# A decoder layer on one core: half 0's output products begin in rooms that half 0 of x leaves, and projections in another order

## The chip, the cores and the metric

The kernel runs on one core of one Trainium2 chip. The metric is the time of one execution on the device, in microseconds (us), as the median of several runs. A core has five engines that work side by side: TensorE (PE) for matrix products, with its own step for loading the stationary operand (PEld in the profile), VectorE (DVE), ScalarE (ACT), GpSimd (POOL), and SyncE (SP), which here only issues transfers (DMAs). Each engine works through its own queue in order and waits on semaphores for the others. SBUF is the memory on the chip, PSUM holds the results of PE in eight banks of 128 x 512 values.

## The reference

One layer for a sequence of 1024 positions and a width of 1024, in float32. What counts for this kernel:

```python
h = rms_norm(x, ln_pre_mix[l])
proj = h @ w_in[l]                      # pool input (256) | q | k | v (12 heads of 64 each)
q, k = rope(q, pos), rope(k, pos)
pool_out = multi_scale_pool(u_pool, w_pool[l], pool_scale[l])
attn_out = dilated_attention(q, k, v)   # windows (128,1), (512,4), (2048,16), merged by softmax denominators
mix = concatenate([pool_out, attn_out]) @ w_out[l]
x = x + rms_norm(mix, ln_post_mix[l])
h = rms_norm(x, ln_pre_ffn[l])
f = (silu(h @ w_gate[l]) * (h @ w_up[l])) @ w_down[l]
x = x + rms_norm(f, ln_post_ffn[l])
```

## The kernel before

**Split numbers.** Every large product is computed three times over split operands: a float32 value is kept as a high part, which PE takes as it is (type fp32r), and the low rest, and high x high, high x low and low x high are added up in PSUM (`PASSES`, three matmuls per step). So each weight tile has to be split before it is used: `wtile` (line 441) loads it, ACT copies the high part and POOL or DVE subtracts (`split`, line 432). The table `we` says for each projection whether DVE or POOL subtracts.

**Halves, pairs and units.** The sequence is cut into two halves of 512 positions (h = 0, 1), the twelve heads into six pairs (p = 0 to 5). One pair and one half is a *unit*: units 0 to 7 are pairs 0 to 3 with both halves in turn, 8 and 9 are pairs 4 and 5 of half 0, and 10 and 11 are pairs 4 and 5 of half 1. Within a unit: `scores` (line 883; eight steps of several products `ps_s<-k,qh` and `ps_s<-k,ql`, half of the steps with every fourth query as stationary operand, "side 1"), `merge` (the weights of the branches), `weigh` (line 973; sixteen scalings of the exponents by DVE, ACT or POOL, by the table `wu`), `turn` (line 1022; transposes through PE, `ps_t<-idt,pp` and `ps_t<-pmt,pp`) and `product` (line 1039; `ps_o<-ptr,v`). The turns may be preceded by transposes of the identity that nobody reads (`ps_t<-idt`); the table `dm` has their number for a unit and a turn.

**Projections as filler.** x, normalised by rows and split, lies in eight tiles `xk[0..7]` of 128 x 2 x 1024 (high and low, all positions). While the units run, the query, key and value projections of the later pairs are the filler of PE: `Fill` (line 717) is a list of steps, and `pull` takes the next step from the list that is current. `await_` (line 694) pulls steps in front of a product whose operands are planned to be late, and the table `x` adds some at single places. A step of a query or key projection (`proj_half`, line 740) is one matmul of 512 columns; a step of a value projection (`v_rows`, line 776) is two matmuls of 256 columns. Split weights lie in tiles `whl`, of which there are two; a value projection needs both, a query or key projection one.

**The order.** A plan in fractions of units is written out by hand: `put(steps, from, to)` spreads steps between two times, such as 10.45 (45 hundredths into unit 10), and `emit` (line 1133) sorts all of them into one program order. PE keeps that order. The other engines' queues are ordered by the framework's planner on the basis of its own estimates. All loads here go through the queue of SP.

**Output products.** The mixed heads of a pair and a half go to memory (`mixd`). `mixed(h)` (line 1242) loads them back as operands k = 0 to 7 (0 and 1 are the pooling part, 2 to 7 the pairs), and `out_proj` (line 1260) multiplies them with the eight output blocks d = 0 to 7. For half 0 they are filler as well, from 10.4487 on: blocks 0 to 2 with operands 2, 3, 4, 5, 0, 1 and 6 up to 11.1989, then operand 7 and the blocks after. Their operands get new tiles in the places of `xk[2]`, `xk[3]`, `xk[6]` and `xk[7]` (`room`, line 1253).

**After the units.** The output products of half 1 and the two norms follow (`chain`, line 1384), then the SwiGLU part, whose matrices are multiplied by blocks with seven products in place of eight (`seven`, line 1567; P1 to P7), and the down projection in the same manner (`down`, line 1834). The last norm needs the mean of the squares of each column: `End` (line 1761) adds squares on DVE into `sq`, keeps the last one apart in `jk`, and `finish` (line 1787) sums both over the partitions by one-column products with `ones` on PE.

Of the kernel before, what the change touches and what calls it, by code (L numbers as in the profile page):

```python
# [35 lines left out]
 'we': (1, 1, 1, 1, 0, 0, 0, 0, 0, 1, 0, 1),  # L36
 'nt0': 0.4937,
 'nt1': 0.5402,
# [3 lines left out]
 'lt': 2.594,  # L42
 'ls': 2.229,
 'lm': 2.364,
 'lw': (3.3, 0.494),
 'nm': 0.0429,
 'n2': -0.0544,
 'n0': 0.2179,
 'n1': 0.3788,
# [24 lines left out]
 'own': {0: {'s0': 0.559,  # L74
             's1': 0.6524,
             'm': 0.8373,
             'w0': 0.8763,
             'w1': 1.2254,
             't0': 1.0833,
             'v0': 1.254,  # L80
# [3 lines left out]
              't1': 1.7207,  # L84
              'v1': 1.9549,
              's1': 0.5395,
              'w0': 0.9014,
              's0': -0.0018,
              'm': 0.6753,
              't0': 0.9791,  # L90
              'v0': 1.0941},
         4: {'m': 0.7142,
             'w0': 0.7313,
             'w1': 0.9854,
             't1': 1.7615,
             'v0': 1.3193,
             'v1': 2.0088,
             's1': 0.4336,
             's0': -0.0464,
             't0': 0.8576},  # L100
         8: {'t1': 1.7086,
             'w1': 0.8589,
             'v0': 1.1186,
             's1': 0.5245,
             'w0': 0.6843,
             'v1': 1.7349,
             'm': 0.612,
             's0': -0.0747,
             't0': 0.7884},
         9: {'s0': -0.0903,  # L110
             't1': 1.7717,
             'v1': 2.0108,
             'w1': 0.9638,
             'w0': 0.6643,
             'v0': 1.1804,
             's1': 0.4339,
             't0': 0.8982,
             'm': 0.543},
         3: {'s0': -0.23,
             't1': 1.7219,  # L120
             'w0': 0.6301,
             'v0': 1.0706,
             's1': 0.6,
             'w1': 1.5566,
             'm': 0.5165,
             'v1': 2.0672},
         1: {'t0': 0.9112,
             'w0': 0.7177,
             'v0': 1.0955,
             'w1': 1.2073,  # L130
             't1': 1.8557,
             'm': 0.5413,
             's0': -0.0064,
             's1': 0.5555,
             'v1': 1.9757},
         10: {'t1': 1.5392,
              't0': 0.9708,
              'v1': 1.9193,
              's1': 0.5967,
              'w1': 1.1507,  # L140
              'v0': 1.1197,
              'w0': 0.6922,
              's0': 0.0404,
              'm': 0.6285},
         6: {'s1': 0.337,
             't1': 1.9316,
             'v0': 1.2209,
             'v1': 2.0292,
             'w1': 1.1291,
             'm': 0.5238,  # L150
             's0': 0.0204,
             'w0': 0.66,
             't0': 0.812},
         7: {'w0': 0.6456,
             't1': 1.8658,
             'm': 0.6436,
             't0': 0.8534,
             's1': 0.4768,
             'v1': 2.0764,
             'v0': 1.1321,  # L160
             'w1': 1.534,
             's0': -0.0044},
         5: {'s1': 0.6462,
             'v1': 2.0851,
             'w1': 1.1017,
             'w0': 0.6388,
             'v0': 1.1233,
             'm': 0.6104,
             't1': 1.8076,
             's0': -0.0052,  # L170
             't0': 1.0214},
         2: {'t1': 1.8214,
             'm': 0.553,
             'w0': 0.7076,
             's0': 0.0298,
             'v1': 2.0119,
             'w1': 1.0298,
             'v0': 1.3523,
             't0': 0.8098}},
 'vt': ((1.029, 1.2775), (2.6607, 3.2018), (4.97, 5.5237), (6.9389, 7.4289), (8.9599, 10.3692), (9.9449, 10.0423)),  # L180
 'pw': 0.2539,
 'pm': (0.8885, (0.8136, 0, 0), (0.8661, 1, 0), (1.035, 0, 1), (1.06, 1, 1)),
# [7 lines left out]
 'lr': (9.8402, 9.7125, 10.0044, 10.2503),  # L190
 'lw0': (9.8553, 10.4888),
 'lc': (12.2353, 12.0824, 11.9907, 12.2417),
 'o0': 10.4487,
 'o1': 11.1989,
 'o2': 12.6671,
 'np': 11.8844,
 'z0': 12.5886,
 'z1': 14.1924,
 'c0': (0.0502, 0.087, 0.2602, 0.595, 0.2709, 0.6193, -0.3497, 0.4162, 0.0467, 0.0316),
 'cut': 5,  # L200
 'ew': (0.1691, 0.4576),
 'c1': (0.115, 0.228, 0.4967, 0.7534, 0.4979, 0.8562, 1.4605, 1.6658, 1.0598, 1.0489),
 'c2': ((1.1162, 1.3893), (1.2471, 1.9662)),
 'e0': ((0.26, 0), (0.42, 0), (0.47, 0.9)),
 'ea': (0, 2, 4),
 'e1': (1.12, 1.25, 1.8, 1.2, 1.5),
 'wu': {(8, 7): 1,
        (6, 10): 1,
# [3 lines left out]
        (6, 7): 0,  # L212
        (0, 0): 0,
        (8, 8): 0,
        (10, 3): 0,
        (0, 1): 0,
        (0, 13): 0,
        (8, 2): 2,
# [8 lines left out]
        (4, 3): 2,  # L227
        (9, 1): 2,
        (10, 11): 2,
        (10, 12): 1,  # L230
        (7, 7): 2,
        (7, 11): 1,
        (10, 6): 1,
        (10, 4): 2,
        (5, 10): 2,
        (10, 15): 2,
        (1, 9): 0,
        (9, 6): 2,
        (2, 13): 2,
        (2, 3): 2,  # L240
        (4, 11): 0,
        (2, 4): 1,
        (2, 9): 2,
        (2, 10): 2,
        (2, 2): 0,
        (8, 6): 2,
        (10, 8): 2,
# [3 lines left out]
        (8, 11): 0,  # L251
# [4 lines left out]
        (8, 5): 0,  # L256
        (8, 10): 2,
        (8, 13): 2,
        (0, 10): 2,
        (6, 14): 2,  # L260
        (0, 5): 2,
        (1, 10): 2,
        (10, 9): 0,
        (4, 14): 2,
        (11, 10): 0,
        (11, 2): 2,
# [6 lines left out]
        (11, 6): 2,  # L273
# [5 lines left out]
        (11, 5): 0,  # L279
# [3 lines left out]
        (6, 6): 2,  # L283
        (10, 13): 2,
        (10, 0): 2,
        (3, 5): 2,
        (3, 9): 2,
        (2, 15): 1,
        (10, 2): 2,
        (1, 5): 0,  # L290
        (10, 7): 2,
        (11, 4): 2,
        (9, 2): 0,
        (9, 14): 0,
        (9, 13): 0,
        (10, 10): 1,
        (2, 8): 2,
        (2, 5): 2,
        (0, 6): 2,
        (0, 15): 1,  # L300
        (0, 8): 0,
        (0, 14): 2,
        (0, 3): 1,
# [73 lines left out]
def hybrid_block(ctx: ExitStack, tc: tile.TileContext, xT, w_in, w_v, w_pv, w_pool, w_out, w_gate, w_up, w_down,  # L377
# [875 lines left out]
    def room(h, n):  # L1253
        if h:
            return fw([P, 2, 2, 512], F32R)
# [763 lines left out]
```

## Time and profile before

| | us |
|---|---|
| median of three runs | 1132.08 |
| the three runs | 1132.82, 1132.08, 1131.9 |
| profiled execution: its own time | 1132.82 |
| its span, first to last instruction | 1131.0 |
| PE busy | 1121.3 |
| DVE, POOL, ACT busy | 779.7, 578.8, 568.0 |

The granted clock of PE was 1.00 throughout. The stages in the profile's time: first projections up to about 85 us, the units from there to about 430 us, norms and the first SwiGLU blocks to about 560 us, then products without a gap up to about 1100 us, and the end.

In the timeline a row has the start and the length in us, the engine, the line, the operation, the tile written and the tiles read, the shape and the number of merged instructions; in brackets stands idle time before it and what ended it. Lengths of matmuls overlap, since they are pipelined, so what one costs is read from start to start. A row of a group has count, busy time, mean ns of one, and idle time of the engine before them. A row of a window has, after its length, busy us and instructions of PE, PEld, DVE, ACT and POOL, the clock, the share of the DMA engines and GB/s. A row of DMA issues has count, KB each and the median us from issue to landing; GB/s there stands in 40 slices of the stretch.

### The profile page before, as it was taken

How to read it: one execution, taken by the hardware profiler on the slowest of the kernel's cores; microseconds unless marked ns; L12 is line 12 of the kernel's file. 1: busy time of each engine (PE TensorE's matmuls, PEld its weight loads, DVE VectorE, ACT ScalarE, POOL GpSimd, SP SyncE). 2: the span in 40 equal slices, each digit the busy share in tenths (PEclk: the TensorE clock that was granted, in tenths of full speed). 3: DMA queues.
4: the chain of work that ended last, by engine and by line, in shares of the span. 5: the costliest groups of instructions: out<-in, count | busy, mean ns of one | idle time of the engine just before them, and what ended most of it. 6: DMA issues, size and time to landing. Idle time of an engine off the chain costs nothing.

```text
span 1131.0 us, 16700 instructions
## 1 busy us (share of the span) xinstructions
PE 1121.3 (99%) x5881; PEld 966.6 (85%) x5881; DVE 779.7 (69%) x1461; ACT 568.0 (50%) x1102; POOL 578.8 (51%) x484
## 2 busy tenths in 40 slices
PE   9999999999999999999999999999999999999997
PEld 7889999999999888878888888888888888888897
DVE  7877878687888666979566755675557365454594
ACT  7457777776787775855323223232232436343430
POOL 0302535363665023232678655976576977655531
PEclk9999999999999999999999999999999999999999
DMA  7324151515137358320345334544454769766642
GB/s 277 127 93 155 57 168 57 167 57 180 48 129 299 130 206 300 131 107 29 141 166 204 139 141 158 218 161 176 162 195 165 273 216 364 248 200 192 204 168 75
DMA packets 85364, 189.01 MB, mean 167 GB/s; under 512 B 8736, under 2 KB 23584, under 8 KB 83872
## 3 DMA queue, kind: packets, MB, share of 16 engines
q1 hardware_dynamic: 84992, 187.68, 47.2%
q8 instruction: 46, 0.75, 0.3%
q14 instruction: 38, 0.31, 0.1%
q10 hardware_dynamic: 288, 0.27, 0.1%
HBM read 134.96 MB, written 52.95 MB: 166 GB/s over the span
## 4 chain that ended last, share of the span: by engine, by line
PE 92%; DVE 2%; POOL 2%; issue 1%; ACT 1%; DMA 1%; DVEq 0%; POOLq 0%; SPq 0%; ACTq 0%
PE ps_pj L382 33%; PE ps_o L382 23%; PE ps_s L382 23%; PE ps_t L382 8%; PE ps_t L385 3%; POOL whl L1610 1%; POOL fw L1610 1%; DVE sq L1365 1%; DVE z L1397 0%; DMA wraw<-in_w_up_dram 0%; DVE z L1398 0%; DMA rw<-in_w_up_dram 0%; POOL whl L437 0%; POOL y L1811 0%; ACT z L1416 0%
## 5 line engine op out<-in xcount | busy, mean ns | idle before, releaser
L382 PE MATMUL ps_pj<-x,whl 128*128 128x512 f32 x480 | 140.0, 406 | 0.0
L1610 POOL TENSOR_TENSOR fw<-rw,fw 128x512 fp32r<-128x512 f32 x74 | 101.2, 1392 | 61.9 <-ACT fw L1608 61.9
L382 PE MATMUL ps_o<-tT,fw 128*128 128x512 f32 x504 | 117.8, 389 | 0.4 <-DVE p L1645 0.4
L382 PEld LDWEIGHTS ps_o<-tT,fw 128*128 128x128 f32 x504 | 94.5, 188 | 20.4 <-DVE p L1645 0.9
L437 POOL TENSOR_TENSOR whl<-wraw,whl 128x512 fp32r<-128x512 f32 x50 | 67.6, 1371 | 83.1 <-ACT whl L433 55.7
L988 POOL TENSOR_SCALAR pp<-pp,wv 128x256 f32<-128x256 f32 (+1 forms) x98 | 47.0, 498 | 116.5 <-DVE wv L966 69.2
L930 ACT ACTIVATE pp<-pp,sx 128x128 f32<-128x128 f32 (+1 forms) x192 | 89.4, 467 | 32.1 <-DVE sx L927 31.4
L1610 POOL TENSOR_TENSOR whl<-rw,whl 128x512 fp32r<-128x512 f32 x42 | 62.1, 1504 | 61.5 <-ACT whl L1608 61.5
L382 PEld LDWEIGHTS ps_pj<-x,whl 128*128 128x128 f32 x480 | 85.0, 189 | 9.8
L1608 ACT ACTIVATE fw<-rw 128x1024 fp32r<-128x1024 f32 x37 | 38.5, 1056 | 92.9 <-DVE rw L1576 32.5
L1757 POOL TENSOR_TENSOR op<-rw,op 128x512 fp32r<-128x512 f32 x38 | 60.3, 1586 | 36.4 <-ACT op L1756 35.0
L1756 ACT ACTIVATE op<-rw 128x1024 fp32r<-128x1024 f32 x38 | 40.2, 1060 | 66.5 <-DMA rw<-bd 29.0
L382 PE MATMUL ps_pj<-whl,x 128*128 128x256 f32 (+1 forms) x432 | 73.0, 303 | 0.0
L1036 DVE TENSOR_TENSOR ptr<-ps_t,ptr 128x512 fp32r<-128x512 f32 (+1 forms) x84 | 55.9, 666 | 17.6 <-ACT ptr L1035 17.1
L382 PE MATMUL ps_pj<-b,fw 128*128 128x512 f32 x264 | 61.6, 389 | 0.0
L382 PEld LDWEIGHTS ps_pj<-whl,x 128*128 128x128 f32 x432 | 59.9, 191 | 1.8
L1035 ACT ACTIVATE ptr<-ps_t 128x512 fp32r<-128x512 f32 (+1 forms) x84 | 48.3, 575 | 23.6 <-PE ps_t L385 20.7
L656 POOL TENSOR_TENSOR rsw<-rsw,sinr 128x512 f32<-128x512 f32 x19 | 24.9, 1312 | 65.6 <-DVE rsw L654 58.7
L382 PEld LDWEIGHTS ps_pj<-b,fw 128*128 128x128 f32 x264 | 49.6, 188 | 10.3
L382 PE MATMUL ps_o<-ptr,v 128*128 128x128 f32 (+1 forms) x472 | 56.2, 254 | 0.0
L382 PEld LDWEIGHTS ps_o<-ptr,v 128*128 128x128 f32 x472 | 52.1, 163 | 3.1 <-DVE ptr L1036 0.3
L382 PE MATMUL ps_s<-k,qh 128*128 128x128 f32 (+1 forms) x192 | 53.4, 290 | 0.0
(342 smaller groups left out, 2926.0 us busy)
## 6 DMA issues: line engine op xcount, KB each, us to landing
rw<-bd SPq DMA_DIRECT2D x77, 256.0 KB, 4.7
v<-vd SPq DMA_DIRECT2D x22, 512.0 KB, 4.7
rw<-wsd SPq DMA_DIRECT2D x44, 256.0 KB, 4.1
rw<-in_w_gate_dram SPq DMA_DIRECT2D x20, 512.0 KB, 3.6
rw<-in_w_up_dram SPq DMA_DIRECT2D x20, 512.0 KB, 4.6
bd<-p SPq DMA_DIRECT2D x33, 256.0 KB, 3.2
rw<-in_w_down_dram SPq DMA_DIRECT2D x33, 256.0 KB, 4.8
fw<-in_w_down_dram SPq DMA_DIRECT2D x16, 512.0 KB, 4.1
```

What stands on the lines that cost most here:

```text
L382: return tc.keep_in_program_order(nc.tensor.matmul(*a, **k))
L385: return tc.keep_in_program_order(nc.tensor.transpose(dst, src, by))
L437: parts.append(eng.tensor_tensor(dst[:, 1, at:at + w], src[:, at:at + w], dst[:, 0, at:at + w].bitcast(F32), ALU.subtract))
L656: pin(eng[0].tensor_tensor(s, s, sinr[:, sl], ALU.mult))
L930: nc.scalar.activation(pt[:, j, lo:], pt[:, j, lo:], AF.Exp, bias=sx[:, 0, side, j, hd, 0:1], scale=-1.0, accum_out=sx[:, 0, side, j, hd, ...
L988: nc.gpsimd.tensor_scalar(pv, pv, un.wv[:, side, j, hd:hd + 1], 1.0, op0=ALU.mult, op1=ALU.mult)
L1035: nc.scalar.activation(ptr[:, 0, :w], t[:, :w], AF.Copy)
L1036: nc.vector.tensor_tensor(ptr[:, 1, :w], t[:, :w], ptr[:, 0, :w].bitcast(F32), ALU.subtract)
L1608: nc.scalar.activation(w[n][:, :, 0], raw[n], AF.Copy)
L1610: low[0] = nc.gpsimd.tensor_tensor(w[n][:, i, 1], raw[n][:, i], w[n][:, i, 0].bitcast(F32), ALU.subtract)
L1756: nc.scalar.activation(w[:, :, 0], raw, AF.Copy)
L1757: nc.gpsimd.tensor_tensor(w[:, 0, 1], raw[:, 0], w[:, 0, 0].bitcast(F32), ALU.subtract)
```

## The change

- **Rooms.** The operands of half 0's output products no longer get new tiles in the places of whole x tiles. They are loaded into halves of them: operands 2 to 5 into the columns of half 0 of `xk[2]`, `xk[3]`, `xk[6]`, `xk[7]`, the others into the columns of half 1. The weights of operands 2 to 5 for blocks 0 and 1 are loaded and split apart (`early`) into half 0's columns of `xk[0]` and `xk[1]`.
- **Start.** The first 24 output products (blocks 0 and 1, operands 2 to 5) are placed at 10.1 to 10.5871, the next 30 at 10.4909 to 11.0568, the rest up to 12.6816. The operand loads are placed at 9.67 to 10.16 (9.71 to 10.25 before). The scores of unit 10 stand at 10.0404 to 10.5472 (to 10.5967 before).
- **Order of projections.** It is a list now (`sq`). All projections end in unit 9; before, nine steps were left for unit 10. The last key and query of half 0 come ahead of the last values.
- **Value weights.** The first use of each half of the value weights also writes the split tiles to memory; later uses load them from there (`v_weights`), as 1 MB a tile.
- **Empty transposes.** `dm` goes from 22 and 1 in unit 9 to 2 in unit 9, 4 in unit 7 and 3 in unit 8.
- **Last norm.** `jk` is only kept apart for half 1. For half 0 the last square is added on DVE, one set of one-column products is left out, and the mean is placed at 0.32 of its stage (0.26 before).
- **SiLU.** A SiLU of one column follows the norm's rows of half 1 in `chain`.
- **Tables.** Most places of the units, the engine of many scalings (POOL 98 to 82, ACT 64 to 76, DVE 30 to 34 in all), and the engine of the splits (`we`) change.

```diff
- 'we': (1, 1, 1, 1, 0, 0, 0, 0, 0, 1, 0, 1),
+ 'we': (0, 0, 1, 1, 0, 0, 1, 0, 0, 0, 0, 0),
...
- 'lr': (9.8402, 9.7125, 10.0044, 10.2503),
- 'lw0': (9.8553, 10.4888),
+ 'lr': (9.6709, 9.7043, 10.1063, 10.1624),
+ 'lw0': (9.8154, 10.3738),
+ 'oe': (10.1, 10.5871),
+ 'le': (10.0102, 9.6845),
...
- 'dm': {(9, 0): 22, (9, 1): 1},
+ 'dm': {(9, 0): 2, (7, 6): 4, (8, 5): 3},
...
+ 'sq': (('k', 1, 0), ('q', 1, 0), ('k', 1, 1), ('q', 1, 1), ('v', 1, 0), ('k', 2, 0), ('q', 2, 0), ('k', 2, 1),
+        ('q', 2, 1), ('v', 1, 1, (2,)), ('v', 1, 1, (0,)), ('q', 3, 0), ('k', 3, 0), ('k', 3, 1), ('q', 3, 1),
+        ('q', 4, 0), ('v', 2, 0, (2,)), ('v', 2, 0, (0,)), ('k', 4, 0), ('k', 4, 1), ('k', 5, 0), ('q', 5, 0),
+        ('k', 5, 1), ('v', 2, 1, (0,)), ('q', 5, 1), ('q', 4, 1), ('v', 2, 1, (2,))),
+ 'fe': (25, 49, 72, 95, 120, 152, 177, 199, 228, 224)}
...
+    def v_weights(n):
+
+        if n not in split_once:
+            split_once[n] = dram.tile([2, P, 2048], F32, name="vws%d" % n)
+            ws = [wtile(w_v[n - 1][kk]) for kk in range(2)]
+            for kk in range(2):
+                nc.sync.dma_start(split_once[n][kk], ws[kk].bitcast(F32).rearrange("p a m -> p (a m)"))
+            return ws
+        ws = [wpool.tile([P, 2, 1024], F32R, name="whl", tag="whl", bufs=2) for kk in range(2)]
+        for kk in range(2):
+            nc.sync.dma_start(ws[kk].bitcast(F32).rearrange("p a m -> p (a m)"), split_once[n][kk])
+        return ws
...
     def room(h, n):
+
+        ks = KS[n]
         if h:
-            return fw([P, 2, 2, 512], F32R)
-        return slot((2, 3, 6, 7)[n], [P, 2, 2, 512], F32R, "m0%d" % n)
+            m["room", n] = t = fw([P, 2, 2, 512], F32R)
+            return {k: t[:, i] for i, k in enumerate(ks)}
+        part = int(n > 1)
...
+        return {k: xk[(2, 3, 6, 7)[n % 2 * 2 + i]][:, :, part * 512:part * 512 + 512] for i, k in enumerate(ks)}
...
+        def early(d):
+            ahead[d] = w = xk[d][:, :, :512]
+            split(w, raw_tile(w_out[d][:, 2:6]), nc.gpsimd)
...
-    st = Fill(st).by(3)
-    put(st[:21], G["o0"], G["o1"])
-    put(st[21:], G["o1"], G["o2"])
+    for steps, lo, hi in ((st[:24], *G["oe"]), (st[24:54], G["o0"], G["o1"]), (st[54:], G["o1"], G["o2"])):
+        put(Fill(steps).by(3), lo, hi)
...
+        def first_rows():
+            sq.rows()
+            if h:
+                nc.scalar.activation(small.tile([P, 1], F32, name="none", tag="none", bufs=1), sq.rb[:, :1], AF.Silu)
...
-                for c in range(n):
+                        stop=(c == n - 1 and lo not in self.jk), skip_group_check=True)
+                for c in range(n if lo in self.jk else 0):
                     mm(sp[:, c:c + 1], self.jk[lo][:, c * P:(c + 1) * P], ones, start=False, stop=(c == n - 1),
...
-            ends[h].add(d, lo, min(hi, 512 - P * h), p in ("P4", "P3") and i == 3)
+            ends[h].add(d, lo, min(hi, 512 - P * h), p == "P3" and i == 3)
```

More of the change, by code (lines that the diff above doesn't have):

```diff
@@ L727, in upto @@
                 self.n += 1
-                self.steps[self.n - 1]()
-                clock[0] += self.each
+                clock[0] += self.steps[self.n - 1]() or self.each
         def by(self, n, total=None):
-            return [lambda i=i: self.upto(i) for i in range(n, (total or len(self.steps)) + 1, n)]
+            total = total or len(self.steps)
+            return [lambda i=min(i, total): self.upto(i) for i in range(n, total + n, n)]
     def pull():
@@ L782, in product @@
                 if "w" not in box:
-                    box["w"] = [wtile(w_v[n - 1][kk]) for kk in range(2)]
+                    box["w"] = v_weights(n)
                 box["ps", t // 2] = bank("pj")
@@ L1075, in product @@
                 else:
-                    into(*(m[h][2][rows, 1, i] for i in range(2)), own, 1.0)
+                    into(*(m[h][7][rows, i] for i in range(2)), own, 1.0)
                 if hd and pr.p < NPAIR - 1:
@@ L1283, in step @@
                 need(("v", 5, h), 2 * len(GROUPS[h]))
-            mk = m[h][k // 2 - 1 if k > 1 else 3][:, k % 2]
-            a, b = PASSES[n]
-            mm(ps, w[:, a, k * P:(k + 1) * P], mk[:, b], start=(first and n == 0), stop=(last and n == 2))
+            mk = m[h][k]
+            mm(ps, w, mk[:, b], start=(first and n == 0), stop=(last and n == 2))
             if last and n == 2:
@@ L1292, in out_proj @@
         ks = (2, 3, 4, 5, 0, 1, 6, 7)
-        order = ([(d, k) for kk in (ks[:7], ks[7:]) for d in range(parts) for k in kk]
-                 + [(d, k) for d in range(parts, NK) for k in ks])
-        return [lambda a=(d, k, k == ks[0], k == ks[-1], n): step(*a) for d, k in order for n in range(3)], weights
+        three = ((0, 1), ks[:4]), ((0, 1), ks[4:6]), ((2,), ks[:6]), ((0,), ks[6:7]), ((1,), ks[6:7]), ((2,), ks[6:7])
+        order = [(d, k) for ds, kk in (three if h == 0 else ((range(parts), ks[:7]),)) for d in ds for k in kk]
+        order += [(d, ks[7]) for d in range(parts)] + [(d, k) for d in range(parts, NK) for k in ks]
+        return [lambda a=(d, k, k == ks[0], k == ks[-1], n): step(*a) for d, k in order for n in range(3)], weights, early
     def zrows(h):
@@ L1308, in hybrid_block @@
         put([step], at, 0)
[L1309 removed]
+    st, weights, early = out_proj(0, 3, None)
+    for d in range(2):
+        put([lambda d=d: early(d)], G["le"][d], 0)
     for d in range(2):
         put([lambda d=d: weights(d)], G["lw0"][d], 0)
[L1312 to L1314 removed]
+    for steps, lo, hi in ((st[:24], *G["oe"]), (st[24:54], G["o0"], G["o1"]), (st[54:], G["o1"], G["o2"])):
+        put(Fill(steps).by(3), lo, hi)
     late = {}
@@ L1453, in block @@
         return B[kh, h]
-    st, weights = out_proj(1, 3, sqs[1][0].add)
+    st, weights, early = out_proj(1, 3, sqs[1][0].add)
     weights(3)
```

331 lines of the change are left out of this document (147 added, 184 removed), and 136 rows, old and new, of the table PRM.

## The prediction

> **What bounds the kernel now.** I read the page first, then what TensorE (PE) waits for, then its timeline where it slows down. The page:
>
> ```profile
> span 1131.0 us, 16700 instructions
> PE 1121.3 (99%) x5881; PEld 966.6 (85%) x5881; DVE 779.7 (69%) x1461; ACT 568.0 (50%) x1102; POOL 578.8 (51%) x484
> ```
>
> PE is busy 99% of the span, so only three things can move the time: products that go, waits of PE, and products that take longer than their columns need. The last kind counts as busy and is seen only in start times. The waits of PE, whole (us in all, times, longest):
>
> ```profile
> PE ps_o L382 <- DVE warm L489: 1.5, 1, 1.5
> PE ps_pj L382 <- ACT q L1638: 1.2, 1, 1.2
> PE ps_o L382 <- DVE p L1645: 0.4, 1, 0.4
> PE ps_o L382 <- DVE dhl L1112: 0.2, 1, 0.2
> PE ps_o L382 <- DVE sq L1365: 0.2, 1, 0.2
> ```
>
> One wait of 1.2 us lies inside the kernel; the first is the start. For the slow products, first a full-rate piece of the chain of waits, then the timeline of PE: a score between projection products in unit 7, and the end of unit 9 with the start of unit 10.
>
> ```profile
> 582.19 5.44 PE ps_o L382 x24
> ```
>
> ```profile
> 277.98 0.28 PE L382 MATMUL ps_s<-k,qh 128*128 128x256 f32 x1
> 278.10 0.40 PE L382 MATMUL ps_pj<-x,whl 128*128 128x512 f32 x1
> ...
> 350.09 2.59 PE L385 MATMUL ps_t<-idt 128*128 128x128 f32 x22
> 352.51 0.60 PE L385 MATMUL ps_t<-idt,pp 128*128 128x128 f32 x4
> 352.87 2.39 PE L382 MATMUL ps_pj<-whl,x 128*128 128x256 f32 x18
> 355.10 0.39 PE L382 MATMUL ps_s<-k,qh 128*128 128x256 f32 x1
> 355.33 0.40 PE L382 MATMUL ps_s<-k,ql 128*128 128x256 f32 x1
> ...
> 362.02 0.40 PE L382 MATMUL ps_s<-k,ql 128*128 128x256 f32 x1
> 362.25 1.33 PE L382 MATMUL ps_pj<-m,whl 128*128 128x512 f32 x5
> ```
>
> A product of 512 columns takes 5.44 / 24 = 0.227 us. A score of 256 columns with a projection product behind it passes in 278.10 - 277.98 = 0.12 us; from 355.10 on, with nothing between them, scores stand 0.23 apart. These are the strided ones (every fourth query); from 355.10 to 362.02 there are 16 of them. Ahead of them stand 22 transposes of the identity, which compute nothing, and one more later. So from 350 to 362 us PE has run out of filler: the projections are used up at 355, and the output products begin at 362.25.
>
> **The change part by part.** *Empty transposes.* 22 take 352.51 - 350.09 = 2.42 us, 0.11 each. The table goes from 23 (unit 9) to 9 (two there, four in unit 7, three in unit 8): 14 fewer, **-1.5 us**. They stood in a wait, so they are gained only if real work stands there instead. It does: the last nine projection steps, the 18 products from 352.87 to 355.10 (2.23 us), now end within unit 9, ahead of that wait, and 20 transposes are 2.2 us. If the weighted exponents came later still, PE would wait as long under another name. Bounds 0 and -1.5; as the covering work fits by the rows, I take -1.5.
>
> *Output products as filler in unit 10.* 24 products for output blocks 0 and 1 (operands 2 to 5, the eight heads of pairs 0 to 3) start at 10.1 instead of 10.45. One of them between two strided scores hides 0.23 - 0.12 = 0.11 us. The unit's scores start at 10.04, a step of four each 0.063, so the first step stays bare: 12 x 0.11, **-1.3 us**. Bounds: 0, if their operands are not there, and 16 x 0.11 = -1.8. Operands and weights now go where half 0 of x stood, which is free once the last product of half 0 (the query of pair 5, early in unit 8) is done. New for this are two 256 KB loads, two ACT copies and four POOL subtractions of weights, with POOL half idle.
>
> *Projections in another order.* In unit 9 strided scores stand beside value products of 256 columns. The timeline of PE there, and in unit 5, beside 512 columns:
>
> ```profile
> 234.19 0.22 PE L382 MATMUL ps_s<-k,qh 128*128 128x128 f32 x1
> 234.26 0.45 PE L382 MATMUL ps_pj<-x,whl 128*128 128x512 f32 x1
> 234.55 0.22 PE L382 MATMUL ps_s<-k,ql 128*128 128x128 f32 x1
> ...
> 326.15 0.34 PE L382 MATMUL ps_s<-k,qh 128*128 128x128 f32 x1
> 326.33 0.45 PE L382 MATMUL ps_pj<-whl,x 128*128 128x256 f32 x2
> 326.62 0.34 PE L382 MATMUL ps_s<-k,ql 128*128 128x128 f32 x1
> ```
>
> Score and filler take 0.47 us with two value products and 0.36 with one projection product, for nearly the same filler work: 0.11 us a score. The new order moves these value products to the end of unit 8 and puts two query projections first in unit 9; unit 6 likewise gets a query projection ahead of its values. In the timeline nine scores of unit 9 and three of unit 6 stand so: 12 x 0.11 = 1.3. A few will still meet a value product; I take **-1.0 us** (bounds 0 and -1.3).
>
> *Value weights split once.* They were loaded and split anew five times, two tiles each. Now two splits also go to memory, and three later uses read them back, 1 MB a tile. So six splits go. Groups of the attention stage (75 to 450 us), then a window of 24 value products, then DMA issues of 75 to 360 us, then two lines of those of 330 to 375 us:
>
> ```profile
> L437 POOL TENSOR_TENSOR whl<-wraw,whl 128x512 fp32r<-128x512 f32 x44 | 58.4, 1348 | 46.5 <-ACT whl L433 46.5
> L433 ACT ACTIVATE whl<-wraw 128x1024 fp32r<-128x1024 f32 x29 | 30.5, 1052 | 2.8 <-PE ps_pj L382 2.2 <-issue 0.3
> ```
>
> ```profile
> 325.91:330.94 5.03, 4.12 (x25) 3.31 (x24) 0.00 (x0) 1.05 (x1) 2.53 (x2) 1.00 0.31 104
> ```
>
> ```profile
> m<-mixd SPq DMA_DIRECT2D x3, 1024.0 KB, 9.0
> wraw<-in_w_v_dram SPq DMA_DIRECT2D x8, 512.0 KB, 3.5
> ...
> GB/s 0 153 328 324 117 124 295 87 246 220 55 350 62 0 0 56 340 148 342 377 382 342 404 375 393 411 419 411 393 386 417 395 419 411 207 300 340 263 333 383
> wraw<-in_w_v_dram SPq DMA_DIRECT2D x1, 512.0 KB, 5.7
> ```
>
> Gone are 12 x 1.35 = 16 us of POOL and 6 us of ACT; both have slack there, so this counts 0. The reload is the price. A projection has two weight rooms, so the second tile can be loaded only when the product group just ahead ends, and it is needed 24 value products later, 5.0 us in that window (the 25th starts at its end). A split was no faster: copy and two subtractions, 1.05 + 2 x 1.35, also follow the release. No row shows 1 MB loaded alone. 512 KB took 3.5 us; half a megabyte more at some 390 GB/s adds 1.3: an estimate of 4.8, just in time. But from about 350 us the queue runs full, and there 1 MB took 9.0 us (4.0 late) and 512 KB 5.7. The third reload falls near that stretch, beside the operand loads that now come earlier: 5.7 + 1.3 = 7.0 would be 2.0 late. Bounds 0 and 3 x 4.0 = +12; I take the first two as on time and half of 2.0 for the third, **+1.0 us**. Behind a reload that waits on SP stand value loads, mixture stores and weight loads, and behind those the value products.
>
> [...]
>
> *A SiLU ahead.* The timeline of ACT and PE at the one inner wait, and the window before it:
>
> ```profile
> 503.53 1.28 ACT L1497 ACT_TABLE_LOAD   x1
> 504.82 0.63 ACT L1497 ACTIVATE p<-p 128x512 f32<-128x512 f32 x1
> ...
> 508.39 0.58 ACT L1638 ACTIVATE q<-ps_pj 128x512 f32<-128x512 f32 x1
> ...
> 509.02 2.34 PE L382 MATMUL ps_pj<-b,op 128*128 128x512 f32 x9 [1.25 <-ACT q L1638]
> ```
>
> ```profile
> 475.00:500.00 25.00, 25.00 (x124) 20.90 (x123) 16.83 (x19) 10.34 (x19) 13.60 (x10) 1.00 0.20 69
> ```
>
> ACT works without a pause from the table load to the copy that PE waits for. A SiLU of one column, some microseconds earlier, where ACT is busy 10.34 of 25 us, takes the 1.28 us out of this row: the copy would end at 507.7, when PE wants its bank. **-1.25 us**, the whole wait. Bounds 0 (another ACT operation moves in between, as several places of this stage are shifted) and -1.25.
>
> *Norm products.* The mean of the last norm, half 0, on PE:
>
> ```profile
> 1067.00 1.03 PE L382 MATMUL ps_t<-ones,p 128*128 128x1 f32 x8
> 1067.89 0.96 PE L382 MATMUL ps_pj<-whl 128*128 128x512 f32 x3
> ```
>
> One set of two is left out: 1067.89 - 1067.00, **-0.9 us**. In its place the last square is added on DVE, and the mean's place goes from 0.26 to 0.32 of the P5 stage (132 products, 30 us), 1.8 us later, which covers one addition. If DVE were late, PE would stand for that addition; bounds 0 and -0.9.
>
> *The rest* (places, the engine of each weighing, splits between DVE and POOL) changes no count of products. The smaller waits above allow 0.8 us, but a shifted place can open as much as it closes: 0.
>
> **Sum.** -1.5 - 1.3 - 1.0 + 1.0 - 1.25 - 0.9 = -4.95. The profiled execution took 1132.82 us (span 1131.0 and 1.8 around it), which is 0.74 above the median of the three runs, 1132.08. From its own time the sum gives 1127.9, against the median **1127.1 us**.
>
> **Rivals.** *The cover is not there* (0.20): the operands or the weights in x's rooms come late in unit 10, so the transposes' time returns as a wait and the scores stay bare. What is left is -1.0 + 1.0 - 1.25 - 0.9 = -2.15: 1129.9. For it speaks the full queue after 350 us; against it, that half 0 of x is free a unit ahead.
>
> *The rooms do not come free by halves* (0.07): if a load into half 0's columns waits for the last reader of the whole tile, the loads start when the projections end, about unit 10.0, and land 9.0 us later, while the first output product stands 0.1 of a unit in, 2.9 us (first scores of units 9 and 10: 326.15 and 355.10). PE keeps its order and waits 6.1. Then the change doesn't do what it says: 1132.08 + 6.1 - 4.95 = 1133.2. Nothing in the rows decides it.
>
> *Slower: the reloads are late* (0.10): each second tile takes the 9.0 us of the loaded queue, PE stands 4.0 us in front of the 25th value product three times: -5.95 + 12 = +6.05, 1138.1. It decides from 2.0 us of lateness each (landing 7.0 us after the release). For it: 1 MB is the size that took 9.0. Against it: two of the three fall where the queue has gaps.
>
> *The clock falls* (0.03): with the transposes gone, a longer wait of PE lets the clock drop. [...]
>
> ```profile
> 1.50 4.63 PE ps_o L382 x10
> ```
>
> 0.46 us a product instead of 0.227. Some 15 products at that rate add 3.5: with the cover gone (-2.15) 1133.4. The longest inner wait here, 1.25 us, left the clock at 1.00. [...]
>
> **How the numbers follow.** Forecast 0.55, the rivals 0.20, 0.07, 0.10 and 0.03, and 0.05 for shifted places that cost or bring 2 us more. The forecast's own range is 1124.5 to 1128.8, from the lower bounds added (-1.5 - 1.8 - 1.3 - 1.25 - 0.9 - 0.8 = -7.55) to 1.7 above. The range goes on to 1132.6 to take in the missing cover and half of the rest; what is left out are the late rooms and the late reloads. Faster means below 1129.8, as 0.2% (2.26 us) is about what a measurement of this kernel tells from no change: the forecast, half of the first rival and part of the rest, 0.69; slower (above 1134.3) the late reloads and some of the rest, 0.12; the same 0.19.
>
> **What would show it.** Right: nine transposes of the identity in place of 23, none at 350 us beyond two; output products between the strided scores of unit 10, with starts 0.35 apart; the table load well ahead of the first SiLU and no wait on the copy at line 1638 (as numbered now); eight rather than sixteen one-column records ahead of the last norm. Wrong: a wait of PE behind a weight reload or an operand load in units 9 and 10, the same score spacing of 0.23, or a new wait in the norm stage that takes the place of the 1.25.

## The result, and the profile after

The changed kernel takes **1125.97 us** (median of 6 runs, 1125.65 to 1126.15), the kernel before in the same session 1132.4 us (6 runs, 1131.85 to 1132.93): ratio 0.9943, 95% interval 0.9931 to 0.9955. It is 6.4 us faster; 5.0 were forecast. In the changed kernel's listing the helpers stand 46 lines further down: L428 and L431 are the products and transposes that were L382 and L385, L1730 is the copy that was L1638.

The page of the changed kernel, its span and its engines:

```profile
span 1124.0 us, 16668 instructions
PE 1115.4 (99%) x5859; PEld 962.9 (86%) x5859; DVE 778.8 (69%) x1465; ACT 567.0 (50%) x1111; POOL 565.4 (50%) x462
```

PE has lost 5.9 us of busy time and the span 7.1. The waits of PE in the changed kernel (us in all, times, longest):

```profile
PE ps_o L428 <- DVE warm L535: 1.5, 1, 1.5
PE ps_o L428 <- DVE ptr L1102: 0.3, 1, 0.3
PE ps_s L428 <- DVE ex L1012: 0.2, 1, 0.2
```

Beyond the start, 0.5 us is left of 2.0. Starts of the same work in both timelines of PE, us from the start of the span, say where the 7.1 us came from:

| start of | before | after | gained since the row above |
|---|---|---|---|
| last value product of the units | 431.90 | 428.37 | 3.53 |
| one-column products of the first norm | 434.84 | 430.96 | 0.35 |
| first product of P1 (b, op) | 502.17 | 498.21 | 0.08 |
| first product with tT | 537.66 | 532.17 | 1.53 |
| last product with tT | 902.76 | 896.53 | 0.74 |
| end of PE | 1124.88 | 1117.76 | 0.89 |

Half of the gain lies in the units. The timeline of PE in the changed kernel at the place that the prediction was about, the end of unit 9 and unit 10:

```profile
347.07 0.49 PE L431 MATMUL ps_t<-idt 128*128 128x128 f32 x3
...
347.64 3.11 PE L428 MATMUL ps_pj<-whl,x 128*128 128x256 f32 x24
...
350.94 0.41 PE L431 MATMUL ps_t<-idt 128*128 128x128 f32 x2
...
352.24 0.40 PE L428 MATMUL ps_s<-k,ql 128*128 128x256 f32 x1
352.47 0.40 PE L428 MATMUL ps_s<-k,qh 128*128 128x256 f32 x1
...
353.29 3.02 PE L428 MATMUL ps_pj<-x,x 128*128 128x512 f32 x12
356.15 0.28 PE L428 MATMUL ps_s<-k,qh 128*128 128x256 f32 x1
356.27 0.40 PE L428 MATMUL ps_pj<-x,x 128*128 128x512 f32 x1
356.51 0.28 PE L428 MATMUL ps_s<-k,ql 128*128 128x256 f32 x1
...
361.83 0.40 PE L428 MATMUL ps_s<-k,qh 128*128 128x256 f32 x1
362.06 0.40 PE L428 MATMUL ps_s<-k,ql 128*128 128x256 f32 x1
```

The operands in x's rooms (`ps_pj<-x,x`) are there at 353.29, without a wait; their loads into half 0's columns were issued at 301.93 and 305.25, while products of half 1 still read x until 350. Twelve products go in one burst, four between four strided scores (0.36 from score to score), and by 361 the 24 are used up: eight strided scores stand bare again, 0.23 apart, as do the four of the first step. Four of unit 10's sixteen are covered, not twelve.

The DMA issues from 75 to 360 us, reloads of the split value weights (count, KB each, median us to landing), and the timeline of PE at the mean of the last norm, half 0, both of the changed kernel:

```profile
whl<-vws SPq DMA_DIRECT2D x6, 1024.0 KB, 4.9
```

```profile
1062.00 0.95 PE L428 MATMUL ps_t<-ones,sq 128*128 128x1 f32 x8
1062.81 0.96 PE L428 MATMUL ps_t<-whl 128*128 128x512 f32 x3
```

No reload kept PE waiting; the last one was issued at 342.35 and landed 4.8 us later, at 347.1, half a microsecond before the 24 value products above begin (347.64). One set of eight one-column products is left where two stood.

The table load that a SiLU needs started at 503.53 before, in front of the copy for which PE waited. The timeline of ACT in the changed kernel:

```profile
486.30 1.28 ACT L1516 ACT_TABLE_LOAD   x1
```

The copy for which PE waited before (L1730 now) starts at 502.22, and PE doesn't wait for it.

### The profile page after: what moved, and what is told of

Read it like the earlier page. It is cut to its first block, busy times and chain, and to the rows that moved or that the text cites. A ratio compares the mean times of both kernels' runs of the same rounds, so it can differ in the third digit from the quotient of the medians.

```text
span 1124.0 us, 16668 instructions
## 1 busy us (share of the span) xinstructions
PE 1115.4 (99%) x5859; PEld 962.9 (86%) x5859; DVE 778.8 (69%) x1465; ACT 567.0 (50%) x1111; POOL 565.4 (50%) x462
## 4 chain that ended last, share of the span: by engine, by line
PE 95%; DVE 3%; ACT 1%; issue 1%; POOL 0%; DVEq 0%; POOLq 0%; ACTq 0%
PE ps_pj L428 33%; PE ps_o L428 25%; PE ps_s L428 24%; PE ps_t L428 9%; PE ps_t L431 3%; ACT pp L996 1%; DVE pp L993 0%; DVE ptr L1102 0%; DVE k L726 0%; POOL y L1903 0%; DVE qh L732 0%; ACT ptr L1101 0%; DVE ex L1012 0%; PE ps_o L431 0%; DVE rsw L700 0%
## 5 line engine op out<-in xcount | busy, mean ns | idle before, releaser
L428 PE MATMUL ps_pj<-x,whl 128*128 128x512 f32 x576 | 169.8, 408 | 0.0
L428 PE MATMUL ps_o<-tT,fw 128*128 128x512 f32 x504 | 117.5, 389 | 0.0
L428 PEld LDWEIGHTS ps_o<-tT,fw 128*128 128x128 f32 x504 | 94.6, 188 | 19.6
L428 PEld LDWEIGHTS ps_pj<-x,whl 128*128 128x128 f32 x576 | 101.1, 189 | 10.7
L1054 POOL TENSOR_SCALAR pp<-pp,wv 128x256 f32<-128x256 f32 (+1 forms) x82 | 42.3, 534 | 115.8 <-DVE wv L1032 68.9
L483 POOL TENSOR_TENSOR whl<-wraw,whl 128x512 fp32r<-128x512 f32 x40 | 54.2, 1374 | 85.3 <-ACT whl L479 55.6
L1849 POOL TENSOR_TENSOR op<-rw,op 128x512 fp32r<-128x512 f32 x38 | 66.2, 1741 | 35.2 <-ACT op L1848 34.2
L428 PE MATMUL ps_pj<-whl,x 128*128 128x256 f32 (+1 forms) x432 | 69.3, 302 | 0.0
L428 PE MATMUL ps_pj<-b,fw 128*128 128x512 f32 x264 | 61.6, 389 | 0.0
L428 PEld LDWEIGHTS ps_pj<-whl,x 128*128 128x128 f32 x432 | 57.9, 190 | 1.5
L428 PEld LDWEIGHTS ps_pj<-b,fw 128*128 128x128 f32 x264 | 49.6, 188 | 10.3
L428 PE MATMUL ps_o<-ptr,v 128*128 128x128 f32 (+1 forms) x472 | 56.1, 254 | 0.3 <-DVE ptr L1102 0.3
L428 PEld LDWEIGHTS ps_o<-ptr,v 128*128 128x128 f32 x472 | 52.0, 163 | 3.3 <-DVE ptr L1102 0.5
L428 PE MATMUL ps_s<-k,ql 128*128 128x128 f32 (+1 forms) x192 | 51.6, 277 | 0.0
```

The costliest lines, as they stand in the source:

```text
L428: return tc.keep_in_program_order(nc.tensor.matmul(*a, **k))
L483: parts.append(eng.tensor_tensor(dst[:, 1, at:at + w], src[:, at:at + w], dst[:, 0, at:at + w].bitcast(F32), ALU.subtract))
L1054: nc.gpsimd.tensor_scalar(pv, pv, un.wv[:, side, j, hd:hd + 1], 1.0, op0=ALU.mult, op1=ALU.mult)
L1849: nc.gpsimd.tensor_tensor(w[:, 0, 1], raw[:, 0], w[:, 0, 0].bitcast(F32), ALU.subtract)
```

## The experiments

Each run is compared with the kernel before on the same chip, whose medians there were 1132.36, 1132.85 and 1133.01 us. Six runs undo one part of the change, one does one part alone, and five move one thing or try what the others left open. The profiled span of the changed kernel, 1124.0, is what their spans stand against. The changed kernel itself was measured in another session, in which the kernel before took 1132.4, so a difference from its 1125.97 can be off by some 0.6 us.

**The SiLU taken out.**

```diff
-            if h:
-                nc.scalar.activation(small.tile([P, 1], F32, name="none", tag="none", bufs=1), sq.rb[:, :1], AF.Silu)
```

> The changed kernel without the SiLU of one column. Theory (the table load stood in front of the copy that PE waits for): the load of 1.28 us comes back between the norm's squares and the first SiLU, and the time rises by 1.2 to 1.6 us over the changed kernel, to about 1127.4; the wait behind the copy of P1 is back. Rival (the shifted places of the norm stage removed the wait, not the SiLU): the load is in the trace, but the time stays within 0.4 us of the changed kernel.

Measured: 1126.2 us (1125.6 to 1126.66), ratio 0.9946 [0.9929, 0.9962], span 1124.2: the changed kernel within 0.2. The timeline of ACT without the SiLU:

```profile
502.53 0.58 ACT L1728 ACTIVATE q<-ps_pj 128x512 f32<-128x512 f32 x1
...
504.15 0.59 ACT L1728 ACTIVATE sq<-ps_pj 128x512 f32<-128x512 f32 x1
504.75 1.28 ACT L1587 ACT_TABLE_LOAD   x1
```

The table load now stands *behind* both copies for which PE waits, at the SiLU that uses it. In the kernel before it stood ahead of the copy for which PE waited 1.25 us. In the changed kernel the shifted places of this stage are enough to remove that wait; the early SiLU had nothing left to remove.

**The SiLU alone, in the kernel before.** The lines that the run above takes out, put into the kernel before and nothing else.

> The kernel before with only the SiLU of one column added. Theory: 1.25 us less than before, about 1131.1, and no wait of PE behind the copy of P1. Rival (it needs the shifted places as well): less than 0.5 us, with another operation of ACT in the place of the load. The small wait behind a DVE product of the first SwiGLU block (0.4 us, some 50 us later) should stay in either case.

Measured: 1134.44 us (1130.93 to 1135.02), ratio 1.0016 [1.0007, 1.0026]. Waits of PE, and windows of its profiled execution, the slowest of ten:

```profile
PE ps_pj L382 <- DVE sq L1365: 1.0, 1, 1.0
```

```profile
529.96:533.37 3.41, 2.40 (x15) 2.13 (x15) 3.31 (x6) 2.08 (x6) 1.01 (x1) 1.00 0.00 0
533.37:536.78 3.41, 3.41 (x9) 2.63 (x9) 2.71 (x6) 2.64 (x5) 0.47 (x1) 0.50 0.00 0
```

The wait on the copy is gone, as the prediction's step said: the SiLU alone does remove it. But PE reaches the next mean earlier and waits 1.0 us there for the squares, and behind this wait the granted clock is 0.50 for 3.41 us: nearly half of that, 1.6 us, is lost, as eight products start 0.43 us apart in place of 0.23. In this execution a wait taken away ahead of another one was not a gain. Another 1.2 us of its 2.2 us of longer span are lost before all this, most at a value load that PE waits for at 102 us. One of the ten executions took 1130.93, near the 1131.1 of the theory; it has no trace.

**The second norm set put back.**

```diff
- 'e0': ((0.32, 0), (0.47, 0), (0.52, 0.9)),
+ 'e0': ((0.26, 0), (0.42, 0), (0.47, 0.9)),
...
-            ends[h].add(d, lo, min(hi, 512 - P * h), p == "P3" and i == 3)
+            ends[h].add(d, lo, min(hi, 512 - P * h), p in ("P4", "P3") and i == 3)
```

> The changed kernel with the last square of half 0 kept apart again, its one-column products back, and the mean at its old place. Theory (PE pays for the products in full): 0.9 us more, about 1126.9, with sixteen one-column records ahead of that norm in place of eight. Rival (they lie in time that PE has anyway): 0.

Measured: 1127.24 us (1126.92 to 1127.37), ratio 0.9955 [0.994, 0.9969], span 1125.0; the waits of PE are those of the changed kernel. The set is worth 1.0 by the spans and 1.3 by the medians.

**Value weights loaded and split anew each time.**

```diff
     def v_weights(n):
 
+        if True:
+            return [wtile(w_v[n - 1][kk]) for kk in range(2)]
```

> The changed kernel with the value weights loaded and split anew each time, as before; nothing is written to memory or loaded back. Theory (reload and split both follow the release by some 5 us, and neither is waited for): within 0.5 us of the changed kernel. Rival 1 (a late reload costs PE time): 0.5 to 2 us less. Rival 2 (the relief of POOL and ACT, 16 and 6 us, is what lets the units run shorter): 1 to 3 us more, with waits of PE behind split weights or weighted exponents.

Measured: 1133.74 us (1131.76 to 1134.7), ratio 1.0009 [1.0, 1.0019]: the whole gain is gone. Waits of PE, and two windows, of the slowest of its ten executions:

```profile
PE ps_s L428 <- DVE ex L1014: 2.7, 3, 2.1
...
PE ps_s L428 <- ACT qh L731: 1.1, 1, 1.1
PE ps_pj L428 <- POOL whl L483: 0.6, 1, 0.6
```

```profile
350.21:353.62 3.41, 3.41 (x19) 3.41 (x18) 2.96 (x8) 2.30 (x6) 3.41 (x4) 0.50 0.88 293
360.45:363.86 3.41, 3.41 (x9) 2.64 (x8) 3.38 (x5) 3.01 (x7) 1.94 (x2) 0.50 0.77 290
```

Exponents, a query copy and a split come late, 4.4 us of waits. Between the merges of units 9 and 10 this run loses 6.7 us: there lie the waits of 2.1 and 1.1 us and, behind them, the two windows at half clock. POOL and ACT have slack as shares of the span, but little here: 3.41 and 1.94 of 3.41 us busy in these windows for POOL, 2.30 and 3.01 for ACT. In the prediction the splits that went counted 0. Whether their own time makes the exponents late, or the other order of the queues that comes with them, this run doesn't tell apart.

**The projections in the order before.**

```diff
- 'sq': (... ('v', 1, 1, (2,)), ('v', 1, 1, (0,)), ('q', 3, 0), ('k', 3, 0), ... ('q', 4, 0), ('v', 2, 0, (2,)), ...
+ 'sq': (... ('v', 1, 1), ('k', 3, 0), ('q', 3, 0), ... ('v', 2, 0), ('k', 4, 0), ('q', 4, 0), ...
```

> The changed kernel with the projections in their old order; all else, the places of the steps too, as changed. Theory (strided scores beside value products cost 0.11 us each, twelve of them come back): 1.0 to 1.3 us more, about 1127.1. Rival (the filler's kind makes no difference in the end): within 0.4 us. If more than 2 us come, something other than the spacing of scores decides, such as a weight tile that comes late in the old order.

Measured: 1131.97 us (1130.57 to 1134.17), ratio 0.9994 [0.9985, 1.0003], profiled span 1129.2. Waits of PE, and the timeline of PE in unit 9:

```profile
PE ps_s L428 <- DVE ex L1012: 2.9, 3, 2.1
...
PE ps_pj L428 <- DMA whl<-vws: 0.9, 1, 0.9
```

```profile
328.29 0.33 PE L428 MATMUL ps_s<-k,qh 128*128 128x128 f32 x1
328.45 0.46 PE L428 MATMUL ps_pj<-whl,x 128*128 128x256 f32 x2
328.75 0.33 PE L428 MATMUL ps_s<-k,ql 128*128 128x128 f32 x1
```

The 0.46 us from score to score is back, the term that the prediction counted. Counted in the timelines of PE from 60 to 450 us, a strided score stands 0.46 from the next, with two value products between them, 24 times in the kernel before, 3 times in the changed kernel and 12 times here. The nine that come back are 9 x 0.11 = 1.0 us. Most of the loss is other: 2.1 us for exponents, and a reload that takes 5.4 us and comes 0.9 us late. So the late reload is real where the order doesn't leave room for it.

**The first 24 output products begin as late as before.**

```diff
- 'oe': (10.1, 10.5871),
+ 'oe': (10.4487, 10.5871),
```

> The changed kernel with the first 24 output products placed from 10.4487 on, where they began before, in place of 10.1. Theory (they fill unit 10's beginning in place of PE's waits and hide strided scores): 1 to 3 us more, as the burst of twelve products that now stands at 353 us becomes a wait, and four more scores stay bare (0.45). Rival (their place does not matter): within 0.4 us.

Measured: 1131.39 us (1130.12 to 1131.92), ratio 0.9989 [0.9979, 0.9998], span 1129.7. Waits of PE, and a window:

```profile
PE ps_t L431 <- DVE ptr L1102: 3.0, 1, 3.0
```

```profile
357.05:363.88 6.83, 6.08 (x30) 6.12 (x31) 4.17 (x13) 6.56 (x23) 1.83 (x2) 0.50 0.57 209
```

Without the burst PE stands at the next turns 3.0 us until DVE has emptied their tile (`ptr`), and the granted clock is 0.50 for 6.83 us from the wait on. What the early products are worth is this wait and the clock, which the prediction didn't name for them, not the bare scores.

**A smaller burst**, to leave filler for the bare scores at 361 us.

```diff
- (10, 's', 1): 8, (10, 's', 2): 7,
+ (10, 's', 1): 3, (10, 's', 2): 2,
```

> The changed kernel with 3 and 2 instead of 8 and 7 products as filler in the second and third step of unit 10, so that the burst of twelve at 353 us gets shorter and filler is left for the eight bare scores at 361 to 364 us. If the burst covers nothing but itself: 8 bare scores less, 8 x 0.11 = -0.9 us at most, -0.5 with half of them: 1125.1 to 1125.6 us, and the trace shows the products between the scores at 361 to 364. Rival (the burst covers the time for which the scores would wait for ScalarE's exp to free their banks): a wait of 1 to 3 us on ex or ps_s appears at 353 to 358 us, and the time is 1127 to 1130 us.

Measured: 1128.24 us (1127.59 to 1128.85), ratio 0.9962 [0.9948, 0.9977], span 1126.5. Timeline of PE:

```profile
353.45 1.87 PE L428 MATMUL ps_pj<-x,x 128*128 128x512 f32 x7
...
359.00 0.52 PE L431 MATMUL ps_t<-pmt,pp 128*128 128x128 f32 x3 [1.57 <-DVE ptr L1102]
```

The rival's case, with another name for the wait than it had: ahead of the turns at 359 stand ten products fewer (2.3 us), and 1.6 us of the wait on `ptr` are back. The saved products run behind it, where nothing waits, and the scores at 363 are bare all the same. What looked like filler wasted in a burst is the filler of that wait.

**The burst ahead of the first step of scores.**

```diff
- 'oe': (10.1, 10.5871),
+ 'oe': (10.03, 10.5871),
```

> The changed kernel with the first output products allowed from place 10.03 on instead of 10.1, so that they can stand between the four bare scores of unit 10's first step too. If the operands are there at 352 us from the span's start: 4 bare scores of 0.23 us become covered ones, 4 x 0.11 = -0.45 us, 1125.5 us, and as much less cover later, so that up to all of it is given back (1126.0). [...]

Measured: 1127.04 us (1126.51 to 1127.39), ratio 0.9952 [0.9937, 0.9966], span 1125.1. The products were ready for it: the burst starts at 351.80 and four of them cover the first step's scores. But the second step is bare now, and the scores and with them the exponents come later: the waits of PE on `ex` rise from 0.2 to 0.8 us. The theory had the cover lost later (up to 1126.0), but not the later exponents; the time lies 1.0 above its range.

**The next 30 products earlier.**

```diff
- 'o0': 10.4909,
+ 'o0': 10.36,
```

> The changed kernel with the next 30 output products from 10.36 on in place of 10.4909, so that filler is left for the eight strided scores that stand bare at 361 to 364 us. If only filler is missing there: 0.5 to 0.9 us less, about 1125.3. If the weights of these products are not split yet (their subtraction ends at 359 us for block 0, later for block 1): PE waits for them, 0 to 3 us more.

Measured: 1128.68 us (1128.07 to 1129.99), ratio 0.9965 [0.9954, 0.9977], span 1127.2: 2.7 slower than the changed kernel by the medians. PE waits 0.9 us on `ex` and 0.8 on operands (`x`, 0.5 by DVE and 0.3 by ACT): the filler reaches operands that aren't there yet.

**The nine empty transposes taken out.**

```diff
- 'dm': {(9, 0): 2, (7, 6): 4, (8, 5): 3},
+ 'dm': {},
```

> The changed kernel without any of the nine empty transposes. Theory (they stand where PE would wait anyway): within 0.4 us of the changed kernel, and PE shows waits of up to 1 us in all in units 7 to 9 where they stood. Rival (each is paid for): 9 x 0.11 = 1.0 us less.

Measured: 1132.97 us (1131.74 to 1134.98), ratio 1.0001 [0.9992, 1.0011]. Nine transposes of 0.11 us are 1.0 us of PE, and without them the kernel is 7.0 us *slower*. Waits of PE, then ACT and POOL from 317 us on, without the transposes:

```profile
PE ps_t L431 <- POOL pp L1054: 2.8, 1, 2.8
PE ps_t L431 <- ACT pp L1050: 2.7, 1, 2.7
```

```profile
317.17 0.60 ACT L1101 ACTIVATE ptr<-ps_t 128x512 fp32r<-128x512 f32 x1 [2.79 <-PE ps_t L431]
317.66 0.19 ACT L1027 ACTIVATE ps_s<-ps_s 128x32 f32<-128x32 f32 x1
...
321.20 2.49 POOL L483 TENSOR_TENSOR whl<-wraw,whl 128x512 fp32r<-128x512 f32 x2 [3.10 <-ACT whl L479]
323.67 2.37 POOL L1054 TENSOR_SCALAR pp<-pp,wv 128x128 f32<-128x128 f32 x6
```

And the changed kernel, the same two engines:

```profile
317.46 0.18 ACT L1027 ACTIVATE ps_s<-ps_s 128x32 f32<-128x32 f32 x1 [3.21 <-PE ps_t L431]
317.55 0.59 ACT L1101 ACTIVATE ptr<-ps_t 128x512 fp32r<-128x512 f32 x1
...
320.05 2.95 POOL L1054 TENSOR_SCALAR pp<-pp,wv 128x128 f32<-128x128 f32 x6 [2.11 <-DVE wv L1032]
322.97 2.54 POOL L483 TENSOR_TENSOR whl<-wraw,whl 128x512 fp32r<-128x512 f32 x2
```

ACT has the merge's small exp and the copy of the transposed rows in the other order, and POOL the scaling of the exponents and the weight split. PE needs the scaled exponents first. The two programs differ by the nine transposes alone, so the other order comes with them. The likely reason is that the transposes carry estimated time for the planner, which orders the queues of the other engines by its estimates; the next run puts part of that order in by hand.

**That order written by hand, without the transposes.**

```diff
- 'dm': {(9, 0): 2, (7, 6): 4, (8, 5): 3},
+ 'dm': {},
...
-            nc.scalar.activation(ptr[:, 0, :w], t[:, :w], AF.Copy)
+            with tc.issue_after(merged[0].ins) if (unit_of[pr.p, h], hd * len(groups) + gi) in HOLD else ExitStack():
+                nc.scalar.activation(ptr[:, 0, :w], t[:, :w], AF.Copy)
```

> The changed kernel without its nine empty transposes, but with ScalarE's two copies of the P rows (turns (7, 6) and (8, 5)) put behind the last merge's small exp by hand, where the changed kernel has them by itself. Theory (the transposes are worth their 6 to 7 us because they steer the order of the other engines' queues): 1125.5 to 1126.8 us, within 0.5 us of the changed kernel; the two waits of 2.8 and 2.7 us on pp are gone and no stretch at half clock follows. Rival (they are worth it by what TensorE does in them, keeping it busy or its clock up): about 1132 to 1133 us, a wait of 1 to 3 us on pp stays and the granted clock falls behind it. Between the two: one of the two waits stays, about 1129.

Measured: 1128.63 us (1127.99 to 1128.67), ratio 0.9963 [0.9949, 0.9977], span 1126.8. Waits of PE, the timeline of POOL, and a window:

```profile
PE ps_t L431 <- ACT pp L1053: 2.0, 1, 2.0
```

```profile
319.93 2.84 POOL L1057 TENSOR_SCALAR pp<-pp,wv 128x128 f32<-128x128 f32 x6 [2.08 <-DVE wv L1035]
```

```profile
354.56:357.97 3.41, 3.41 (x10) 2.67 (x9) 2.44 (x7) 3.39 (x11) 1.75 (x2) 0.50 0.82 306
```

The middle case of the expectation. With the exp ahead of the copy POOL scales first again and the 2.8 us wait is gone: 4.3 of the 7.0 us come back with no transpose at all, so there the transposes work by the order. The second wait stays at 2.0 us, with half clock behind it. The hand-written order doesn't reach it, and whether it too is one of order was not tried.

**The 23 empty transposes of the kernel before taken out.**

```diff
- 'dm': {(9, 0): 22, (9, 1): 1},
+ 'dm': {},
```

> The kernel before without its 23 empty transposes at unit 9. If they only fill a wait that is there anyway: 1132.0 to 1132.8, no change; the trace shows a wait of 2.2 to 2.4 us in their place and the granted clock stays at 1.00. If they were longer than the wait: up to 1.5 us less, 1131. If they keep the clock: the wait is followed by 3.41 us at half clock, as in the runs in which the changed kernel was made to wait, and the time is 1.7 us more, 1134.0 to 1134.5.

Measured: 1134.04 us (1132.04 to 1135.69), ratio 1.0011 [1.0002, 1.0021]; the profiled execution is the fastest of ten, with a span of 1130.2 against 1131.0. Waits of PE in it, and the loads of the mixed heads there (first and last start at the end of the row):

```profile
PE ps_pj L382 <- DMA m<-mixd: 2.0, 1, 2.0
...
PE ps_t L385 <- POOL pp L988: 1.2, 1, 1.2
```

```profile
L1249 SPq DMA_DIRECT2D m<-mixd x4: 326/368/421, 348.3 to 364.5; - x4
```

The wait in place of the 22 transposes is 1.2 us long, not 2.2 to 2.4. But the four transposes behind it run slower (0.78 us in place of 0.36), so from the start of the products ahead (`ps_o<-ptr,v`, 349.74 before, 349.15 here) to the value products behind (352.87 and 351.65) only 0.6 us came free: some 1.8 of the 2.42 us covered a real stall. The 0.6 was spent again in unit 10. A load of mixed heads is issued at 364.5, where the kernel before had its last at 362.0, and PE waits 2.0 us for it. The shorter span, 0.8 us, was won in the first 18 us, where the profiled executions of all these kernels differ by up to 1.2 us. The clock stayed at 1.00 behind both waits in this execution; the mean granted clock of the ten goes from 0.999 in the fastest (1132.04) to 0.996 in the slowest (1135.69), so in others it probably did not. This mean takes in the end of the kernel too, where the clock falls after the last product (in the changed kernel it is 0.68 on the mean of the last 6.2 us).

## Why the prediction was right, and where its steps were not

The forecast was 1127.1, measured 1125.97, inside the forecast's own range; the time came out better by 1.1. Yet several terms were off in ways that cancel, so it is partly luck that the number is this close.

- **Empty transposes, -1.5.** Fourteen fewer, hardly a wait in their place (0.36 us of the weight load, for exponents, at 351.47), and real work where the prediction put it: 24 value products at 347.64 in unit 9. The step took all 2.42 us of the 22 as a wait; 1.8 of it was. And it priced a transpose by PE's time alone; taking out those that are left costs 7.0 us, 4.3 of it by the order of the other queues.
- **Output products as filler, -1.3.** The mis-sized term. Four of sixteen bare scores are covered, 4 x 0.11 = -0.45. The step took the 24 products as spread over the steps of scores by their planned places; 12 of them go in one burst at 353. What they do there is another thing: they fill a wait of 3.0 us on `ptr`. The kernel before had its last 18 value products at this place, so against it that is no gain; it is what lets the projections end in unit 9 without a new wait.
- **Projections in another order, -1.0.** The mechanism is there, and larger than the step had it. It counted twelve scores, in units 6 and 9; by the count above, 24 intervals of 0.46 before and 3 after, 21 x 0.11 = -2.3 went, with all the changed places together. The old order alone brings nine of them back, 1.0 us of the 6.0 that it loses.
- **Value weights split once, +1.0.** Measured 0. The three second tiles, which have a deadline, took 4.8 us each, the estimate of the prediction, and the deadline of 5.0 was met; the queue stood idle ahead of the third (342.35). First tiles, which nobody waits for yet, took up to 7.7. Half of 2.0 for the third reload was too much. The other side was not 0: with the splits back, this kernel takes 7.8 us more. The "slack" of POOL was read from its share of the span, not from that stretch.
- **The units together.** Predicted -1.5 - 1.3 - 1.0 + 1.0 = -2.8, measured -3.53. By the sizes above, -1.5 - 0.45 - 2.3 = -4.25 and 0 for the reloads; some 0.7 us was lost again in the units, at places that were not followed.
- **SiLU ahead, -1.25.** The stretch gained 1.53 and the wait on the copy went, with the table load at 486.30 as the step said. But the step had one cause where there are two: the SiLU alone removes the wait, and so do the shifted places, which put the table load behind the copies. Without the SiLU the time is 0.2 longer, with ranges that overlap. The bound "another ACT operation moves in between, as several places are shifted" saw the shift and not its sign.
- **Norm products, -0.9.** Measured -0.89 at the end of PE, 1.0 to 1.3 by putting them back. Right.
- **The rest, 0.** Two of the small waits went: 0.35 at the first norm's squares and 0.74 on DVE's `p`, -1.1. Start to start they cost more than the 0.2 and 0.4 us of idle time in the list of waits, as did the 1.25 on the copy (1.53).

By this count: -3.53 - 0.35 - 0.08 - 1.53 - 0.74 - 0.89 = -7.1 of span between the two profiled executions, against -4.95 in the sum: 1.2 us more from the small waits, 0.7 from the units, 0.3 at the SiLU. The forecast comes nearer than that only because it also took off 0.74 for the distance of the profiled execution from the median of three. That is no part of the change; over six runs the distance is 0.4, and the profiled execution of the changed kernel lies 0.1 below its own median.

Of the **rivals**, the cover was there and the rooms did come free by halves: the operands were loaded while half 1 was still being read, and the first output product at 353.29 waits for nothing. A late reload exists only in the old order (0.9 us). The clock didn't fall in the changed kernel before its last product: 1.00 up to 1117.76 us. The chance of 0.03 for that rival was too low for this kernel: in five of the twelve experiments the profiled execution shows it, always at a wait. Its price, 0.46 us a product, was read from the first products of the kernel before, and no run shows a lower clock there: the granted clock is 1.00 from 1.50 to 6.10 us. The windows at 0.50 show 0.43 for a product of 512 columns.

The parts don't add up. Undone one at a time, six of them cost 0.2 (SiLU), 1.3 (norm), 5.4 (early start), 6.0 (order), 7.0 (transposes) and 7.8 us (reloads), 27.7 together, for a change worth 6.4. In the four large ones the trace shows a wait that the changed kernel doesn't have, in three of them with half clock behind it; that their places and orders were fitted to the part that is missing is a reading, not a measurement. A sum over parts was still a fair forecast here because the changed kernel has no such wait left.

## What to carry to other kernels

Where PE is the bound and its order is fixed, ask of every filler which wait lies under it and how long it is: filler moved off a slow product may be all that covers a late copy. An instruction that computes nothing can still decide in which order a planner puts the other engines' work, so its removal is priced by the new queues, not by its own time. And price a new wait of PE of a microsecond or more at itself plus, in case the clock falls, the 1.6 us that the run with the SiLU alone lost by it: in the fourteen profiles of this case six of twelve such waits inside the kernel came with half clock.

## What the runs showed of the hardware

**Half clock at waits of 1 to 3 us.** The stretches above with a granted clock of 0.50 inside the kernel are 3.41 us long, once 6.83, twice that; the two in the run with the splits start 10.24 us apart, three times 3.41. Within them products of 512 columns start 0.43 us apart, not 0.23 (SiLU alone, exp first, splits again). Bare strided scores start 0.22 to 0.24 apart there (late start) and 0.23 at full clock, so they lose next to nothing; in the kernel before, loading their stationary operand takes 0.33 us, and 0.19 us without the stride. PE lost the clock after a wait of 1.0 us (SiLU alone), 2.0 (exp first) and 3.0 (late start), while it kept it behind 1.57 (smaller burst), behind 2.0 in the kernel before without transposes, behind 2.1 in the old order (products of 512 columns start 0.24 to 0.27 us apart behind it) and behind 2.7 in the kernel without the nine transposes. The windows that lie right ahead of such a stretch, and one that kept the clock, in the kernel without the nine transposes:

```profile
322.92:326.33 3.41, 2.20 (x14) 2.06 (x15) 1.60 (x3) 1.80 (x5) 3.12 (x7) 1.00 0.26 77
326.34:329.75 3.41, 3.41 (x18) 3.31 (x17) 1.78 (x6) 2.86 (x9) 1.43 (x2) 0.50 0.09 27
...
353.65:357.06 3.41, 1.54 (x14) 1.40 (x13) 2.94 (x8) 2.87 (x5) 3.41 (x4) 1.00 0.50 147
357.06:360.47 3.41, 2.61 (x16) 2.48 (x17) 2.76 (x10) 3.41 (x10) 3.41 (x5) 1.00 1.02 312
```

PE was busy 2.20 of 3.41 us and lost the clock, and busy 1.54 and kept it. So in these runs neither the length of the wait nor the busy time of the 3.41 us ahead decides it alone; what does was not found.
